# Stacking the last 16 keys' value products, spreading the rotary keys over 128 partitions and issuing the branch loads later, in a four-mixer decoder layer on one core

## The chip, the core and the metric

The kernel runs on 1 core of one Trainium2 chip. The metric is the device time of one execution in microseconds (us). Three runs of the kernel before took 991.82, 991.32 and 989.41 us (median 991.32). A difference of about 0.3% is what a measurement of this kernel can tell from none.

## The reference, cut to what matters

One decoder layer on 1040 positions: 16 learned meta tokens, then 1024 of the sequence, each of width 1024. `NM` is 16, `L` is 1040, `H` is 8 heads.

```
h = rms_norm(x);  z = h @ w_in                       # all branch inputs and gates
y_a = pool_mixer(...)  @ w_out_pool
y_b = attention(...)   @ w_out_mla                   # 8 heads, 64 + 32 rotary dims, values of 64
y_c = conformer_conv(...) @ w_out_conf
y_d = short_conv(...)  @ w_out_sc
m = sum_i sigmoid(g_i) * y_i
out = (x + rms_norm(m @ w_o))[16:]
```

The attention is causal: query q sees the meta tokens and the sequence up to itself. The last 16 keys of a block of 512 queries are seen by its last 16 queries alone, because the meta tokens shift keys against queries by 16. The rotary part of the key (32 dims) is one for all heads.

Every float32 product is made of three TensorE products of split operands: with x = xh + xl and w = wh + wl it is wh·xh + wh·xl + wl·xh (the halves are of type float32r). So each block of values costs three products, too.

## The kernel before, in words

**Stages.** (1) About 0 to 645 us: x is normalised and transposed, and w_in is multiplied in "units" of seven products each with DVE, ACT and POOL evacuating; between the units the pumps advance the other work (convolutions, pooling, query, key and value projections, weight splits), whose results go to DRAM. (2) 645 to 858 us: attention, 8 heads in two halves of 512 queries, and between its products the 48 "fills", the output projections of the three other branches. (3) The rest: the attention's output projection and w_o.

**Order of the work.** The program is recorded first, and `Plan.flush` (line 355) then deals it out: each engine takes, at each planned time, the ready operation with the lowest priority number. Costs and landing times are its own estimates; `plan.behind()` (line 268) makes an operation wait in the plan for the last recorded TensorE operation, or for a given one; nothing on the chip waits for that, it only sets the order on the queue. `plan.ahead(n)` moves priorities. SP issues nearly all loads in this order, one after the other, and an issue whose semaphore isn't there holds all behind it.

**Attention** (`attend`, line 1438). For each block `j` of 128 keys: three score products into a bank of tag "s" (five banks), a mask on DVE, Exp on ACT into `p32`, a split into a high part (ACT copy) and a low part (POOL subtraction) in `pt`, and three value products into the one bank "o": `v_[:, j, :P]` (64 values, high part, and 64 ones, which sum the rows) with the high and the low part, then `v_[:, j, P:]` (low part of the values) with the high part (lines 1463 to 1465). For the last block the same happens on 16 keys and 16 queries. The maximum of each row is put into four extra rows of the query tile `qt`, by a transpose and a DVE multiplication with `negd` (line 1432); scores of a half can't start before this.

**Between stages 1 and 2.** The last unit's four gate outputs go through three buffers `z` and are stored to `th` by POOL (line 752, `g == 30`). DVE's last evacuation, `z<-ps_pc`, needs the buffer of the first of them, so it waits for that store to land; DVE's two `qt` operations stand behind it. Meanwhile SP loads: queries, masks, keys and values of two heads, and the first branch's operands `bo` (two of 1 MB, `load_bo(0)`, line 1524), weights `whl` and gates `th` for the first fill.

**Rotary keys** (`task_kv`, line 1207): on 32 partitions of 1040 columns, two products with the cosine and sine tables, a sum, and a split, POOL doing four of the five operations. At the same time DVE halves parts of the parameter table `par` (line 904), in place.

Of the kernel before, what the change touches and what calls it, by code (L numbers as in the profile page):

```python
# [21 lines left out]
F32 = mybir.dt.float32  # L22
# [8 lines left out]
P = 128  # L31
# [40 lines left out]
def f(ap):  # L72
    return ap.bitcast(F32)
# [385 lines left out]
def trunk_kernel(ctx, tc, a):  # L459
# [56 lines left out]
    q_dram = [dram.tile([H, QK, 2, 512], F32R, name=f"q{c}") for c in range(2)]  # L516

    k_dram = [dram.tile([P, 2, L], F32R, name=f"k{g}") for g in range(4)]
    kr_dram = dram.tile([32, 2, L], F32R, name="kr")

    v_dram = [dram.tile([4, P, 9, 192], F32R, name=f"v{g}") for g in range(2)]
    l_dram = [dram.tile([NT], F32, name=f"l{h}") for h in range(H)]
    r_dram = [dram.tile([NT], F32, name=f"r{h}") for h in range(H)]

    mask_dram = [dram.tile([P, P], F32, name=f"mask{i}") for i in range(2)]
    negd_dram = dram.tile([4, 4, P], F32, name="negd")
# [27 lines left out]
    def t4(shape, dt=F32, name="t4"):  # L554
        return tp.tile(shape, dt, tag="t4", bufs=4, name=name)
# [345 lines left out]
    PE.transpose(pt[:, :NPAR], prow[:NPAR, :], ident[:NPAR, :NPAR])  # L901
    DVE.tensor_copy(par[:, :NPAR], pt[:, :NPAR])
    for r0, r1, n in ((R_DW, R_DW, 62), (R_GB, R_GB, 32), (R_HLB, R_LB, 2)):
        DVE.tensor_scalar(par[:, r0:r0 + n], par[:, r1:r1 + n], 0.5, None, op0=ALU.mult)

# [38 lines left out]
    def task_consts():  # L944

        for i in range(2):
            mask = w1([P, P], name="mask")
            causal(mask, 1 - 2 * i)
            ld(mask_dram[i], mask)
        t = t4([4, L], name="kone")  # L950
        POOL.memset(t, 1.0)
        ld(ones_dram, t)
        t = t4([4, 4, P], name="negd")
        POOL.memset(t, -1.0)
        POOL.affine_select(out=t, in_=t, compare_op=ALU.is_equal, fill=0.0,
                           base=0, pattern=[[-1, 4], [0, P]], channel_multiplier=1)
        ld(negd_dram, t)
        yield

    def k_rows(k_, h, part):  # L960

        e = h % 2
        ld(k_[:64], part(k_dram[h // 2][64 * e:64 * (e + 1)]))
        if h < 2:
            for r in range(2):
                ld(k_[64 + 16 * r:80 + 16 * r], part(kr_dram[16 * (r ^ e):16 * (r ^ e) + 16]))

    def row_maxima(c, mx, q_, k_, mask, bank):

# [236 lines left out]

    def task_kv():

        k0, k1, cs = t4([32, L], name="kr0"), t4([32, L], name="kr1"), t4([32, L], name="kcs")
        for k_, r0, i in ((k0, 0, 0), (k1, 32, 1)):  # L1210
            ld(k_, z_dram["kr"][r0:r0 + 32, :])
            ld(cs, a["trig"][i][:32, :])
            mul(POOL, k_, k_, cs)
            cs = t4([32, L], name="kcs2") if i == 0 else None
        add(POOL, k0, k0, k1)
        yield
        kh = t4([32, L], F32R, name="krh")
        copy(kh, k0)
        ld(kr_dram[:, 0], kh)
        kl = t4([32, L], F32R, name="krl")  # L1220
        sub(POOL, kl, k0, f(kh))
        ld(kr_dram[:, 1], kl)
# [12 lines left out]
        yield  # L1235
        for g in range(4):
            wk = w1([P, P], name="wk")
            ld(wk.rearrange("p (h c) -> p h c", c=64),
               w_ukv[:, 2 * P * g:2 * P * (g + 1)].rearrange("p (h c) -> p h c", c=P)[:, :, :64])
            whl = w1([P, 2, P], F32R, name="wkhl")  # L1240
            split(whl[:, 0], whl[:, 1], wk)
            yield
            for n0, n in CH_L:
                ps = bank()[:, :n]
                PE.matmul(ps, whl[:, 0], ch[:, n0:n0 + n], start=True, stop=False)
                PE.matmul(ps, whl[:, 0], cl[:, n0:n0 + n], start=False, stop=False)
                PE.matmul(ps, whl[:, 1], ch[:, n0:n0 + n], start=False, stop=True)
                hl = t4([P, 2, 348], F32R, name="khl")[:, :, :n]
                copy(hl[:, 0], ps)
                sub(DVE, hl[:, 1], ps, f(hl[:, 0]))  # L1250
                ld(k_dram[g][:, :, n0:n0 + n], hl)
                yield
        for g in range(2):
            wv = w1([P, 4, 64], name="wv")
            ld(wv, w_ukv[:, 4 * P * g:4 * P * (g + 1)].rearrange("p (h c) -> p h c", c=P)[:, :, 64:])
            whl = w1([P, 2, 256], F32R, name="wvhl")
            split(whl[:, 0].rearrange("p (h c) -> p h c", c=64), whl[:, 1].rearrange("p (h c) -> p h c", c=64), wv)
            yield
            for j in range(9):
                n = P if j < 8 else NM  # L1260
                ps = bank()[:n, :256]
                s_ = slice(P * j, P * j + n)
                PE.matmul(ps, ch[:, s_], whl[:, 0], start=True, stop=False)
                PE.matmul(ps, ch[:, s_], whl[:, 1], start=False, stop=False)
                PE.matmul(ps, cl[:, s_], whl[:, 0], start=False, stop=True)
                p3 = ps.rearrange("p (h c) -> p h c", c=64)
                hl = t4([P, 4, 192], F32R, name="vhl")[:n]
                POOL.memset(f(hl[:, :, 64:128]), 1.0)
                copy(hl[:, :, :64], p3)
                sub(DVE, hl[:, :, 128:], p3, f(hl[:, :, :64]))  # L1270
                ld(v_dram[g][:, :n, j].rearrange("h p c -> p h c"), hl)
                yield
# [113 lines left out]
    negd = qk.tile([4, 4, P], F32, name="negd")  # L1386
    NA = QK + 4
    qt = {}

# [3 lines left out]

    load_q(0, 0)
    kt = [qk.tile([NA, 2, LK], F32R, name=f"kt{i}") for i in range(2)]
    vt = [qk.tile([P, 9, 192], F32R, name=f"vt{i}") for i in range(2)]
    for t, src in ((maskS, mask_dram[0]), (maskT, mask_dram[1]), (negd, negd_dram),
                   *((kt[i][QK:NA, 0, :L], ones_dram) for i in range(2))):
        ld(t, src)

# [8 lines left out]
    def load_v(h):  # L1409
        v_ = vt[h % 2]  # L1410
        v = v_dram[h // 4][h % 4]
        ld(v_[:, 0:8].rearrange("p j c -> p (j c)"), v[:, 0:8].rearrange("p j c -> p (j c)"))
        ld(v_[:NM, 8], v[:NM, 8])

    def maxima(h, c):

        q_, k_ = qt[h, c], kt[h % 2]  # L1420
# [11 lines left out]
        DVE.tensor_tensor(q_[QK:NA, 0, :].rearrange("p (r n) -> p r n", n=P),  # L1432
                          pm[:4, :P].unsqueeze(1).to_broadcast([4, 4, P]), negd, op=ALU.mult)
        yield

    ol = {}
# [1 line left out]
    def attend(h, c):  # L1438
# [4 lines left out]
        for j in range(nj):  # L1443
# [15 lines left out]
            pt_ = at.tile([P, 2, 512], F32R, tag="pt", bufs=4, name="pt")[:kn, :, :n]  # L1459
            ACT.activation(p32, s, AF.Exp)  # L1460
            split(pt_[:, 0], pt_[:, 1], p32)
            o = po[:, lo_ - 512 * c:]
            PE.matmul(o, v_[:kn, j, :P], pt_[:, 0], start=(j == 0), stop=False, skip_group_check=True)
            PE.matmul(o, v_[:kn, j, :P], pt_[:, 1], start=False, stop=False, skip_group_check=True)
            PE.matmul(o[:64], v_[:kn, j, P:], pt_[:, 0], start=False, stop=(j == nj - 1), skip_group_check=True)
            yield
        if c == 0:
            ol[h] = at.tile([P, 2, 512], F32, tag="ol", bufs=2, name="ol")
# [47 lines left out]
    def fills():  # L1516
# [322 lines left out]
```

## Time and profile before

| What | us |
|---|---|
| three runs | 991.82, 991.32, 989.41; median 991.32 |
| the profiled execution, its own time | 990.85 |
| its span, from the first to the last instruction | 989.0 |
| TensorE (PE) busy | 969.4 (98%) |
| VectorE (DVE), GpSimd (POOL), ScalarE (ACT) busy | 696.8, 692.7, 444.0 |
| mean granted TensorE clock | 0.993 |

The 1.85 us between span and time lie around the program. A row of the timeline gives start, length, engine, tile written and tiles read, shape and count; what stands in brackets is the idle time before and what ended it. L353 is the line that issues all planned operations, so groups are told apart by tile names. PEld is the weight load of a product; matmuls are pipelined, so the start of one to the start of the next is its price, not its own length.

### The profile page before, as it was taken

How to read it: one execution, taken by the hardware profiler on the slowest of the kernel's cores; microseconds unless marked ns; L12 is line 12 of the kernel's file. 1: busy time of each engine (PE TensorE's matmuls, PEld its weight loads, DVE VectorE, ACT ScalarE, POOL GpSimd, SP SyncE). 2: the span in 40 equal slices, each digit the busy share in tenths (PEclk: the TensorE clock that was granted, in tenths of full speed). 3: DMA queues.
4: the chain of work that ended last, by engine and by line, in shares of the span. 5: the costliest groups of instructions: out<-in, count | busy, mean ns of one | idle time of the engine just before them, and what ended most of it. 6: DMA issues, size and time to landing. Idle time of an engine off the chain costs nothing. (4 is left out here: it accounts for less than half of the span.)

```text
span 989.0 us, 15388 instructions
## 1 busy us (share of the span) xinstructions
PE 969.4 (98%) x5095; PEld 824.6 (83%) x5095; DVE 696.8 (70%) x1109; ACT 444.0 (45%) x898; POOL 692.7 (70%) x630
## 2 busy tenths in 40 slices
PE   9999999999999999999999999989999999999996
PEld 8998899889888887888887888868888888788885
DVE  5948966979988965555365677236776687799747
ACT  7644243344344554554344344356455554224631
POOL 5848665558777787996599788345468795647956
PEclk9999999999999999999999999989999999999998
DMA  7144567667778687777647787778778674772634
GB/s 253 35 113 129 170 203 233 217 210 243 218 261 266 191 249 218 230 228 223 183 133 215 239 273 257 198 276 280 202 184 271 187 193 129 253 249 90 202 112 170
DMA packets 134551, 202.30 MB, mean 205 GB/s; under 512 B 20262, under 2 KB 81309, under 8 KB 133704
## 3 DMA queue, kind: packets, MB, share of 16 engines
q1 hardware_dynamic: 125496, 184.54, 60.8%
q10 hardware_dynamic: 8656, 15.74, 4.4%
q8 instruction: 40, 0.66, 0.3%
q0 software_dynamic: 320, 1.05, 0.3%
q14 instruction: 39, 0.32, 0.1%
HBM read 128.48 MB, written 72.81 MB: 204 GB/s over the span
## 5 line engine op out<-in xcount | busy, mean ns | idle before, releaser
L353 PE MATMUL ps_pb<-T,S 128*128 128x512 f32 (+2 forms) x792 | 171.6, 358 | 2.0 <-DVE u L353 2.0
L353 PE MATMUL ps_pa<-B,A 128*128 128x512 f32 (+2 forms) x792 | 170.4, 360 | 0.0
L353 PEld LDWEIGHTS ps_pb<-T,S 128*128 128x128 f32 x792 | 134.5, 189 | 23.7 <-DVE u L353 2.4
L353 PEld LDWEIGHTS ps_pa<-B,A 128*128 128x128 f32 x792 | 134.6, 188 | 22.8 <-issue 1.4
L353 POOL TENSOR_TENSOR S<-ss,S 128x512 fp32r<-128x512 f32 x84 | 114.5, 1376 | 49.0 <-ACT S L353 48.7
L353 POOL TENSOR_TENSOR A<-raw,A 128x512 fp32r<-128x512 f32 x84 | 114.6, 1370 | 39.2 <-ACT A L353 37.6
L353 POOL TENSOR_TENSOR pt<-p,pt 128x512 fp32r<-128x512 f32 (+4 forms) x112 | 105.6, 967 | 49.4 <-PE ps_s L353 31.5
L353 DVE TENSOR_TENSOR u<-ps_pb,u 128x512 f32<-128x512 f32 (+2 forms) x66 | 40.3, 611 | 78.2 <-PE ps_pb L353 71.6
L353 DVE SCALAR_TENSOR_TENSOR ps_w<-conv,par,ps_w 128x512 f32<-128x512 f32 x116 | 87.2, 752 | 2.6
L353 PE MATMUL ps_y<-bo,whl 128*128 128x512 f32 x288 | 87.1, 409 | 0.0
L353 PE MATMUL ps_pc<-B,S 128*128 128x512 f32 (+1 forms) x396 | 86.4, 359 | 0.0
L353 PE MATMUL ps_pd<-T,A 128*128 128x512 f32 (+2 forms) x396 | 85.2, 359 | 0.0
L353 PE MATMUL ps_pc<-T,S 128*128 128x512 f32 (+1 forms) x396 | 84.2, 358 | 0.0
L353 ACT ACTIVATE S<-ss 128x512 fp32r<-128x512 f32 x84 | 50.4, 627 | 68.5 <-DVE ss L353 37.3
L353 ACT ACTIVATE p<-ps_s 128x512 f32<-128x512 f32 (+4 forms) x112 | 49.4, 442 | 60.2 <-PE ps_s L353 34.9
L353 PEld LDWEIGHTS ps_pc<-B,S 128*128 128x128 f32 x396 | 67.0, 188 | 11.1 <-issue 0.5
L353 PEld LDWEIGHTS ps_pd<-T,A 128*128 128x128 f32 x396 | 67.0, 188 | 10.6
L353 PEld LDWEIGHTS ps_pc<-T,S 128*128 128x128 f32 x396 | 66.8, 189 | 10.7
L353 PE MATMUL ps_o<-pt,vt 128*128 128x512 f32 (+4 forms) x336 | 73.5, 329 | 0.4 <-ACT ol L353 0.4
L353 PE MATMUL ps_s<-qt,kt 100*128 100x512 f32 (+4 forms) x336 | 70.5, 333 | 0.3 <-DVE qt L353 0.3
L353 PEld LDWEIGHTS ps_o<-pt,vt 128*128 128x128 f32 (+1 forms) x336 | 54.4, 171 | 15.1 <-issue 1.3
L353 DVE TENSOR_TENSOR z<-ps_pc,u 128x512 f32<-128x512 f32 (+1 forms) x66 | 40.2, 609 | 37.3 <-PE ps_pc L353 27.3
(271 smaller groups left out, 1933.1 us busy)
## 6 DMA issues: line engine op xcount, KB each, us to landing
raw<-in_w_in_dram SPq DMA_DIRECT2D x52, 512.0 KB
th<-th SPq DMA_DIRECT2D x32, 512.0 KB
th<-z ACTq DMA_DIRECT2D x60, 256.0 KB
v<-vhl SPq DMA_DIRECT2D x16, 384.0 KB
qt<-q SPq DMA_DIRECT2D x16, 384.0 KB
vt<-v SPq DMA_DIRECT2D x8, 768.0 KB
bo<-bo SPq DMA_DIRECT2D x6, 1024.0 KB
kt<-k SPq DMA_DIRECT2D x8, 520.0 KB
```

Source lines behind the costliest of these rows:

```text
L353: getattr(self.handle[o["eng"]], o["op"])(*map(real, o["args"]), **{k: real(v) for k, v in o["kw"].items()})
```

## The change

Five edits. (a) In `attend`, the last 16 keys are taken apart from the full blocks: their probabilities are put into a tile `pz` of 80 rows, high part in rows 0 to 15, low part in 32 to 47, high part again in 64 to 79, zero between; the values into a tile `vs`, rows as they belong to these; one product of 80 rows takes the place of three of 16. ACT makes two copies where it made one. `vs` is loaded by three small loads for each head in place of one, and zeroed once by a load. (b) The rotary keys are worked on as 128 partitions of 260 columns, and stored as `[2, 32, L]`. (c) The halved parameters are read from the PSUM bank of the transpose, not from `par` itself. (d) `negd` is gone; the extra key rows are -1 and the diagonal is taken from `ident`. (e) `load_bo(0)` and the first fill's loads are planned behind the last TensorE operation recorded so far, and the second and third fill's behind the first fill's first product.

```diff
-    kr_dram = dram.tile([32, 2, L], F32R, name="kr")
+    kr_dram = dram.tile([2, 32, L], F32R, name="kr")
...
-        DVE.tensor_scalar(par[:, r0:r0 + n], par[:, r1:r1 + n], 0.5, None, op0=ALU.mult)
+        DVE.tensor_scalar(par[:, r0:r0 + n], pt[:, r1:r1 + n], 0.5, None, op0=ALU.mult)
...
-        k0, k1, cs = t4([32, L], name="kr0"), t4([32, L], name="kr1"), t4([32, L], name="kcs")
+        def rows32(x):
+            return x.rearrange("p (c n) -> (p c) n", c=4)
+        k0, k1, cs = (t4([P, L // 4], name=x) for x in ("kr0", "kr1", "kcs"))
         for k_, r0, i in ((k0, 0, 0), (k1, 32, 1)):
-            ld(k_, z_dram["kr"][r0:r0 + 32, :])
-            ld(cs, a["trig"][i][:32, :])
+            ld(k_, rows32(z_dram["kr"][r0:r0 + 32, :]))
+            ld(cs, rows32(a["trig"][i][:32, :]))
             mul(POOL, k_, k_, cs)
...
-    vt = [qk.tile([P, 9, 192], F32R, name=f"vt{i}") for i in range(2)]
+    vt = [qk.tile([P, 8, 192], F32R, name=f"vt{i}") for i in range(2)]
+    vs = [qk.tile([NS, 2, P], F32R, name=f"vs{i}") for i in range(2)]
+    pz = [at.tile([NS, NM], F32R, name=f"pz{i}") for i in range(3)]
...
+        e = v[:NM, 1:9].rearrange("p (c j) d -> p c j d", j=4)[:, :, 3]
+        for r, w in ((0, slice(0, P)), (32, slice(0, P)), (64, slice(P, 192))):
+            ld(vs[h % 2][r:r + NM, :, :w.stop - w.start], e[:, :, w])
         ld(v_[:, 0:8].rearrange("p j c -> p (j c)"), v[:, 0:8].rearrange("p j c -> p (j c)"))
-        ld(v_[:NM, 8], v[:NM, 8])
...
+            if kn == NM:
+                x = pz[(2 * h + c) % 3]
+                copy(x[:NM], p32)
+                copy(x[64:], p32)
+                sub(POOL, x[32:32 + NM], p32, f(x[:NM]))
+                PE.matmul(o, vs[h % 2][:, c], x, start=False, stop=True, skip_group_check=True)
+            else:
...
-        bos = {}
-        load_bo(0)
+        bos, begun = {}, []
+        with plan.behind():
+            load_bo(0)
...
-                with plan.behind() if d + bi else nullcontext():
+                with plan.behind(begun[0] if 0 < d + bi < 3 else None):
                     whl = wtile(fp, wname, d, 0)
                     ld(th, th_dram[8 * gi + d])
+                begun.append(len(plan.ops))
```

The plan deals the work out anew, so rows move on all engines from about 80 us on. Three places matter in what follows.

SP at the start of attention, from the second head's keys (`kt_6900`, now `kt_6905`) on. Before:

```order
L353 DMA kt_6900<-kr 16x2x1040 x2
L353 DMA bo<-bo_5246 128x2048
L353 DMA bo<-bo_5777 128x2048
L353 DMA whl<-w_out_pool_715 128x512
L353 DMA th<-th_3932 128x1024
L353 DMA vt_6931<-v_2504 128x1536
L353 DMA vt_6931<-v_2504 16x192
L353 DMA qt<-q_5072 96x1024
L353 DMA whl<-w_out_pool_1051 128x512
```

And now:

```order
L354 DMA kt_6905<-kr 16x2x1040 x2
L354 DMA vs_6903<-v_2483 16x2x128 x2
L354 DMA vs_6903<-v_2483 16x2x64
L354 DMA vt_6931<-v_2483 128x1536
L354 DMA qt<-q_5254 96x1024
L354 DMA bo<-bo_5184 128x2048
L354 DMA bo<-bo_5695 128x2048
L354 DMA whl<-w_out_pool_715 128x512
L354 DMA th<-th_3935 128x1024
L354 DMA qt<-q_4075 96x1024
```

The branch operands stood ahead of the second head's values; now they stand behind them and behind the fourth query load, which waits for a query buffer to come free.

PE at the same place: `ps_s<-ident,mrs` are the transposes for the first head's row maxima, `ps_s<-qt,kt` scores, `ps_s<-kt,qt` the second head's row maxima, `ps_o` value products, `ps_y<-bo` a fill. Before:

```order
L353 MATMUL ps_s<-ident,mrs 4x128 x2
L353 MATMUL ps_s<-kt_6900,qt 128x144
L353 MATMUL ps_s<-kt_6900,qt 128x272
L353 MATMUL ps_s<-kt_6900,qt 128x400
L353 MATMUL ps_s<-qt,kt_6898 128x512 x3
L353 MATMUL ps_s<-qt,kt_6898 128x400 x3
L353 MATMUL ps_s<-qt,kt_6898 128x272 x3
L353 MATMUL ps_s<-qt,kt_6898 128x144 x3
L353 MATMUL ps_s<-qt,kt_6898 16x16 x3
L353 MATMUL ps_o<-pt,vt_6905 128x512
L353 MATMUL ps_y<-bo,whl 128x512 x2
```

And now:

```order
L354 MATMUL ps_s<-ident,mrs 4x128 x2
L354 MATMUL ps_s<-qt,kt_6899 128x512 x3
L354 MATMUL ps_s<-qt,kt_6899 128x400 x3
L354 MATMUL ps_s<-qt,kt_6899 128x272 x3
L354 MATMUL ps_s<-qt,kt_6899 128x144 x3
L354 MATMUL ps_s<-qt,kt_6899 16x16 x3
L354 MATMUL ps_s<-kt_6905,qt 128x144
L354 MATMUL ps_o<-pt,vt_6913 128x512
L354 MATMUL ps_s<-qt,kt_6899 128x512 x5
L354 MATMUL ps_o<-pt,vt_6913 128x512
```

The three row maxima ahead of the first scores have moved behind them, and the first fill, which came 10 rows behind the transposes, now comes 50 rows behind them, after 77 products.

DVE in stage 1, around the halving of `par` (`u<-ps_pb` is the evacuation for which a unit's next product waits). Before:

```order
L353 COPY par<-ps_x 128x111
L353 TENSOR_SCALAR par<-par 128x62
L353 SCALAR_TENSOR_TENSOR z<-z 128x272
L353 TENSOR_TENSOR z<-ps_pc,u_1059 128x256
L353 SCALAR_TENSOR_TENSOR z<-z 128x256
L353 TENSOR_SCALAR par<-par 128x32
L353 TENSOR_TENSOR u_1187<-ps_pb,u_1163 128x256
L353 TENSOR_SCALAR par<-par 128x2
```

And now:

```order
L354 COPY par<-ps_x 128x111
L354 TENSOR_SCALAR par<-ps_x 128x62
L354 TENSOR_SCALAR par<-ps_x 128x32
L354 TENSOR_SCALAR par<-ps_x 128x2
L354 SCALAR_TENSOR_TENSOR z<-z 128x272
L354 TENSOR_TENSOR z<-ps_pc,u_1059 128x256
L354 SCALAR_TENSOR_TENSOR z<-z 128x256
L354 TENSOR_TENSOR u_1184<-ps_pb,u_1165 128x256
```

All three halvings now follow the copy at once, and none stands beside the two `u` evacuations of the next unit.

More of the change, by code (lines that the diff above doesn't have):

```diff
@@ L47 @@
 LH = 512 + NM
+NS = 5 * NM
 LK, LR = 1088, 576
@@ L525, in trunk_kernel @@
     mask_dram = [dram.tile([P, P], F32, name=f"mask{i}") for i in range(2)]
-    negd_dram = dram.tile([4, 4, P], F32, name="negd")
+    zero_dram = dram.tile([NS, 2 * P], F32, name="zero")
     ones_dram = dram.tile([4, L], F32, name="ones4")
@@ L950, in task_consts @@
         t = t4([4, L], name="kone")
-        POOL.memset(t, 1.0)
+        POOL.memset(t, -1.0)
         ld(ones_dram, t)
[L953 to L957, printed above, removed]
+        t = t4([NS, 2 * P], name="zero")
+        POOL.memset(t, 0.0)
+        ld(zero_dram, t)
         yield
@@ L965, in k_rows @@
             for r in range(2):
-                ld(k_[64 + 16 * r:80 + 16 * r], part(kr_dram[16 * (r ^ e):16 * (r ^ e) + 16]))
+                ld(k_[64 + 16 * r:80 + 16 * r], part(kr_dram[:, 16 * (r ^ e):16 * (r ^ e) + 16].rearrange("s p n -> p s n")))
     def row_maxima(c, mx, q_, k_, mask, bank):
@@ L1207, in task_kv @@
     def task_kv():
-        k0, k1, cs = t4([32, L], name="kr0"), t4([32, L], name="kr1"), t4([32, L], name="kcs")
+        def rows32(x):
+            return x.rearrange("p (c n) -> (p c) n", c=4)
+        k0, k1, cs = (t4([P, L // 4], name=x) for x in ("kr0", "kr1", "kcs"))
         for k_, r0, i in ((k0, 0, 0), (k1, 32, 1)):
-            ld(k_, z_dram["kr"][r0:r0 + 32, :])
-            ld(cs, a["trig"][i][:32, :])
+            ld(k_, rows32(z_dram["kr"][r0:r0 + 32, :]))
+            ld(cs, rows32(a["trig"][i][:32, :]))
             mul(POOL, k_, k_, cs)
-            cs = t4([32, L], name="kcs2") if i == 0 else None
+            cs = t4([P, L // 4], name="kcs2") if i == 0 else None
         add(POOL, k0, k0, k1)
         yield
-        kh = t4([32, L], F32R, name="krh")
+        kh = t4([P, L // 4], F32R, name="krh")
         copy(kh, k0)
-        ld(kr_dram[:, 0], kh)
-        kl = t4([32, L], F32R, name="krl")
+        ld(rows32(kr_dram[0]), kh)
+        kl = t4([P, L // 4], F32R, name="krl")
         sub(POOL, kl, k0, f(kh))
-        ld(kr_dram[:, 1], kl)
+        ld(rows32(kr_dram[1]), kl)
         yield
@@ L1385, in trunk_kernel @@
     maskS, maskT = (qk.tile([P, P], F32, name=n) for n in ("maskS", "maskT"))
-    negd = qk.tile([4, 4, P], F32, name="negd")
     NA = QK + 4
@@ L1395, in trunk_kernel @@
     kt = [qk.tile([NA, 2, LK], F32R, name=f"kt{i}") for i in range(2)]
-    vt = [qk.tile([P, 9, 192], F32R, name=f"vt{i}") for i in range(2)]
-    for t, src in ((maskS, mask_dram[0]), (maskT, mask_dram[1]), (negd, negd_dram),
+    vt = [qk.tile([P, 8, 192], F32R, name=f"vt{i}") for i in range(2)]
+    vs = [qk.tile([NS, 2, P], F32R, name=f"vs{i}") for i in range(2)]
+    pz = [at.tile([NS, NM], F32R, name=f"pz{i}") for i in range(3)]
+    for t in pz:
+        POOL.memset(f(t), 0.0)
+    for t in vs:
+        ld(t.rearrange("p c n -> p (c n)"), zero_dram)
+    for t, src in ((maskS, mask_dram[0]), (maskT, mask_dram[1]),
                    *((kt[i][QK:NA, 0, :L], ones_dram) for i in range(2))):
@@ L1432, in maxima @@
         DVE.tensor_tensor(q_[QK:NA, 0, :].rearrange("p (r n) -> p r n", n=P),
-                          pm[:4, :P].unsqueeze(1).to_broadcast([4, 4, P]), negd, op=ALU.mult)
+                          pm[:4, :P].unsqueeze(1).to_broadcast([4, 4, P]),
+                          ident[:4, :4].unsqueeze(2).to_broadcast([4, 4, P]), op=ALU.mult)
         yield
@@ L1458, in attend @@
             p32 = at.tile([P, 512], F32, tag="p32", bufs=3, name="p32")[:kn, :n]
-            pt_ = at.tile([P, 2, 512], F32R, tag="pt", bufs=4, name="pt")[:kn, :, :n]
             ACT.activation(p32, s, AF.Exp)
-            split(pt_[:, 0], pt_[:, 1], p32)
             o = po[:, lo_ - 512 * c:]
-            PE.matmul(o, v_[:kn, j, :P], pt_[:, 0], start=(j == 0), stop=False, skip_group_check=True)
-            PE.matmul(o, v_[:kn, j, :P], pt_[:, 1], start=False, stop=False, skip_group_check=True)
-            PE.matmul(o[:64], v_[:kn, j, P:], pt_[:, 0], start=False, stop=(j == nj - 1), skip_group_check=True)
+            if kn == NM:
[5 more added lines that the diff above has]
+            else:
+                pt_ = at.tile([P, 2, 512], F32R, tag="pt", bufs=4, name="pt")[:, :, :n]
+                split(pt_[:, 0], pt_[:, 1], p32)
+                PE.matmul(o, v_[:, j, :P], pt_[:, 0], start=(j == 0), stop=False, skip_group_check=True)
+                PE.matmul(o, v_[:, j, :P], pt_[:, 1], start=False, stop=False, skip_group_check=True)
+                PE.matmul(o[:64], v_[:, j, P:], pt_[:, 0], start=False, stop=False, skip_group_check=True)
             yield
```

## The prediction

> **What bounds the kernel now.** I read the page first, for the busy shares, then the busy time by stretch.
>
> ```profile
> span 989.0 us, 15388 instructions
> PE 969.4 (98%) x5095; PEld 824.6 (83%) x5095; DVE 696.8 (70%) x1109; ACT 444.0 (45%) x898; POOL 692.7 (70%) x630
> ...
> 645.00:657.40 12.40, 8.56 (x30) 6.52 (x29) 4.77 (x14) 3.45 (x7) 2.96 (x4) 0.72 1.02 395
> 657.40:820.00 162.60, 162.60 (x867) 135.49 (x866) 112.92 (x283) 91.41 (x208) 118.64 (x119) 1.00 0.73 211
> ```
>
> TensorE is the bound: 969.4 of 989.0 us, and in steady attention 162.60 of 162.60, at full clock. There a product removed is time removed, and other engines' work counts only where PE waits for it. The first stretch is the exception: PE is busy 8.56 of 12.40 us, and the clock (third number from the end) is 0.72. So next I read PE's waits, and around these the timeline.
>
> ```profile
> PE ps_s L353 <- DVE z L353: 3.4, 1, 3.4
> PE ps_pb L353 <- DVE u L353: 2.0, 2, 1.5
> ```
>
> Of some 20 us in which PE isn't busy, these two waits are those that the change touches; the others lie at the program's start and end. 0.3% of the time is 3.0 us, and that is what a measurement can tell from no change.
>
> **Part A, the last 16 keys: -4.2 us.** Sixteen halves of attention each lose three products of 16 rows and gain one of 80. The last unit of the program shows the price, and a product of 128 rows with a single column bounds the new one.
>
> ```profile
> 851.66 0.33 PE L353 MATMUL ps_o<-pt,vt 16*128 16x16 f32 x2
> 851.92 0.50 PE L353 MATMUL ps_y<-bo,whl 128*128 128x512 f32 x1
> ...
> L353 PE MATMUL ps_x<-ones,sqk 128*128 128x1 f32 x16 | 1.9, 240 | 0.0
> L353 ACT ACTIVATE pt<-p 16x16 fp32r<-16x16 f32 x16 | 3.4, 214 | 4.3 <-PE ps_o L353 4.1
> ```
>
> Two small products start at 851.66 and the next work at 851.92, so each holds PE for 0.13 us, whatever its 16 columns. One with 128 rows and one column takes 1.9 / 16 = 0.12, so rows cost nothing either, and I price the new one at 0.13. Two fewer in each of 16 halves: 16 x 2 x 0.13 = 4.2 us, all on the path, since PE is full there. Bounds: 3.2 if the 80-row one took 0.19, and 4.5 if 0.11. ACT's second copy adds 16 x 0.21 = 3.4 us to an engine at 45%. The one product must wait for POOL's difference, as the second of the three did, so that wait is not new. Two more small loads a head are issued on SP, ahead of loads of a later head: at no cost while those are a head early (their price if that cover went is in Part C).
>
> **Part B, rotary keys and parameters: -2.0 us.**
>
> ```profile
> 77.72 4.96 POOL L353 TENSOR_TENSOR kr<-kr,kcs 32x1040 f32<-32x1040 f32 x2
> 82.75 2.43 POOL L353 TENSOR_TENSOR kr<-kr,kr 32x1040 f32<-32x1040 f32 x1
> 85.15 0.73 POOL L353 TENSOR_TENSOR whl<-wraw,whl 128x256 fp32r<-128x256 f32 x1
> 86.79 2.45 POOL L353 TENSOR_TENSOR krl<-kr,krh 32x1040 fp32r<-32x1040 f32 x1 [0.25 <-PE ps_pc L353]
> ...
> 73.83 0.27 DVE L353 COPY par<-ps_x 128x111 f32<-128x111 f32 x1
> 77.95 2.37 DVE L353 TENSOR_SCALAR par<-par 128x32 f32<-128x32 f32 x1
> 80.58 2.13 DVE L353 TENSOR_SCALAR par<-par 128x2 f32<-128x2 f32 x1
> ...
> 80.71 1.69 PE L353 MATMUL ps_pb<-T,S 128*128 128x256 f32 x12 [1.53 <-DVE u L353]
> 91.64 1.58 PE L353 MATMUL ps_pb<-T,S 128*128 128x256 f32 x11 [0.48 <-DVE u L353]
> ```
>
> A multiplication of 32 columns by a number takes DVE 2.37 us, and one of 2 columns 2.13, just while POOL works on the 1040 rotary columns; the copy of 111 columns from PSUM took 0.27. DVE's evacuation `u` stands behind the first, and PE waits 1.53 us for it; behind `krl`, another `u` is late and PE waits 0.48. Now the three halvings read PSUM and come early, each bounded by the copy's 0.27, and POOL's four operations have 260 columns, priced by the 256-column row at 0.73 in place of 2.43 to 2.48. Both waits should go: 1.53 + 0.48 = 2.0 us. What is late next is PE itself: no other wait of this place stands among its waits. Bounds: 0 if the new order puts another slow DVE operation before a `u`, and 2.5 with what DVE's delay costs inside a product. Keys are needed only in attention, so the smaller packets of their loads and stores (1040 bytes a row in place of 4160) are hidden by hundreds of us.
>
> **Part C, the start of attention: -0.6 us.** These rows are SP's, POOL's, DVE's and PE's.
>
> ```profile
> 636.95 1.23 SPq L353 DMA_DIRECT2D bo<-bo  x2
> 640.88 3.21 SPq L353 DMA_DIRECT2D vt<-v  x2
> 653.72 0.32 SPq L353 DMA_DIRECT2D qt<-q  x1
> ...
> 639.34 0.76 POOL L353 DMA_DIRECT2D th<-z  x1 [11.35 <-ACT z L353]
> 650.25 0.54 POOL L353 DMA_DIRECT2D th<-z  x1 [6.42 <-ACT z L353]
> ...
> 648.50 0.69 DVE L353 TENSOR_TENSOR z<-ps_pc,u 128x512 f32<-128x512 f32 x1 [8.23 <-DMA th<-z]
> 649.23 1.28 DVE L353 TENSOR_TENSOR qt<-ps_s,negd 4x512 fp32r<-4x512 f32 x2
> ...
> 642.10 2.88 PE L353 MATMUL ps_pc<-B,S 128*128 128x512 f32 x12
> 644.82 0.38 PE L353 MATMUL ps_s<-ident,mrs 128*4 128x128 f32 x2
> 645.40 0.47 PE L353 MATMUL ps_s<-kt,qt 96*128 96x144 f32 x2 [0.20 <-PE ps_s L353]
> 649.25 0.45 PE L353 MATMUL ps_s<-kt,qt 96*128 96x400 f32 x1 [3.38 <-DVE z L353]
> 649.97 3.73 PE L353 MATMUL ps_s<-qt,kt 100*128 100x512 f32 x15 [0.26 <-DVE qt L353]
> ```
>
> The chain is: POOL's store of the first `z`, issued at 639.34, has landed at 648.50, 9.2 us later; then DVE's `z` (0.69) and first `qt` (half of 1.28), and at 649.97 the first scores, 1.5 us behind the landing. PE has nothing from about 645.9 to 649.25. Then the clock falls. The next fence has the stretches of it, and the last products of the program for comparison; ahead of them the load queue's packets between 640 and 645.7, and between 643.3 and 651 those of both queues (q0 is POOL's).
>
> ```profile
> q1 hardware_dynamic: 282, 1.28, 102.1%
> ...
> q1 hardware_dynamic: 294, 2.08, 73.5%
> q0 software_dynamic: 215, 0.75, 23.9%
> ...
> 643.50:646.93 3.43, 2.18 (x11) 1.37 (x9) 0.00 (x0) 0.00 (x0) 0.33 (x1) 1.00 0.95 326
> 646.93:650.34 3.41, 0.83 (x3) 0.52 (x4) 1.80 (x3) 0.72 (x1) 0.09 (x1) 1.00 0.99 413
> 650.34:657.17 6.83, 6.83 (x24) 5.52 (x23) 2.97 (x12) 2.73 (x6) 2.87 (x4) 0.50 1.03 384
> 977.99:981.40 3.41, 1.42 (x12) 1.22 (x11) 3.38 (x7) 1.59 (x6) 2.62 (x3) 1.00 0.41 154
> 981.40:989.00 7.60, 0.00 (x0) 0.00 (x0) 4.41 (x8) 0.14 (x2) 2.86 (x3) 0.50 0.65 242
> ```
>
> PE had 0.83 of 3.41 us to do, and the next 6.83 ran at 0.50: 3.4 us lost on top of the wait. At the end 1.42 of 3.41 was followed by half clock too, while 2.18 of 3.43 wasn't.
>
> What the change moves: `bo`, `whl` and `th` go behind the second head's values and a query load that SP could not issue before 653.72. So 2 MB less stand in the queue when the store goes out. Up to 645.7 the queue holds the same keys as before, and the store's packets don't show there at all (q1 alone, at 102.1%); its wait for a first packet is thus not made by `bo`. What `bo` can cost is the store's own passage after that: some 0.75 MB of q0 for three stores beside 73.5% of q1. I take 1.0 us off the landing: a store of 0.25 MB took a third of 7.7 us, 2.6, at a share of 23.9%, and with twice the share would take 1.3.  Bounds: 0, and 3 if the store waits for the whole queue to drain. So the first scores start at about 649.0. The three row maxima that used the gap now come later; at full clock a column costs 2.72 us / (12 x 512) (twelve products from 642.10 to 644.82), and their 816 columns 0.4 us. Net -1.0 + 0.4 = -0.6. From 645.3 to 649.0 PE then has nothing for 3.7 us, as long as before, so I leave half clock in.
>
> The Trainium skill, "DMA: Bandwidth & Descriptors", section on queues, rings and completion order, says that a DMA engine takes turns between the queues with work, packet by packet. By it a store is never held behind a full load queue, and holding `bo` back would gain next to nothing: the sum would end 1.0 us later. The trace agrees only in part, since q0 shows nothing until 645.7.
>
> New wait: the first fill. Between the first score and it stand 77 products of 27,384 columns: 12 us at full clock, 15.5 with half clock. Its loads go out behind the query load, 3.75 us after the first score (653.72 against 649.97); 0.4 + 2.0 + 0.25 MB at 2.08 MB in 7.7 us is 9.8, with 1 us to land 14.6. Hidden, by about 1 us; full clock would leave 2.6 us open, less what it saves. Part A's two extra loads of the first heads are issued here too, at half of 1.23 us each by `bo`'s row: up to 1.2, beside a queue that is full.
>
> **The sum.** The profiled execution took 990.85 us (span 989.0, 1.85 around it), 0.47 under the median of 991.32. 990.85 - 4.2 - 2.0 - 0.6 = 984.0.
>
> **The rivals.**
>
> *The clock stays up.* If the store lands by 646, the first scores start at 647.5, 2.4 us earlier, and the gap is 2.2: by the rows above not enough to drop the clock unless one window holds it all. It saves 2.4 - 0.4 + 3.4 = 5.4 in place of 0.6: 979.2. For it: 2 MB fewer in the queue. Against it: q0's absence before 645.7, when the queue is as before; the fourth store, issued at 650.25 beside a full queue too, has nothing of `bo` to blame. Chance 0.22. The Trainium skill, "TensorE: Matmul & The Clock Gate", section "Why this matters for your kernels", puts the limit at PE-idle gaps of about 3 us; by that rule a gap of 2.2 would keep the clock up, and my 3.7 would not.
>
> *The branch operands come late (the other side).* PE's queue is in order, so a first fill without operands stops everything behind it, scores too. The margin is 1 us. The page's rate by slices shows how it could go:
>
> ```profile
> GB/s 253 35 113 129 170 203 233 217 210 243 218 261 266 191 249 218 230 228 223 183 133 215 239 273 257 198 276 280 202 184 271 187 193 129 253 249 90 202 112 170
> ```
>
> At the 129 GB/s of a slice in attention, 2.65 MB take 20.5 us in place of 9.8: 10.7 later, 9.7 beyond the margin, and half clock again, 3.4: 984.0 + 13.1 = 997.1. It decides from 1 us of lateness, and cancels the whole gain at a lateness of 4.4 (3.4 + 3.4 = 6.8). Against it: around 650 the queue moves 384 to 413 GB/s. Chance of more than +3 us against before 0.04, of cancelling most 0.08.
>
> *It doesn't do what it says.* PE may wait at the small product for POOL in place of issuing three, or B's waits may return elsewhere in the new order; at half of A and B, 990.85 - 3.1 = 987.7. Against it: PE has no such wait in 162.60 us. Chance 0.08.
>
> **How the numbers follow.** Forecast 0.58 (984.0), clock 0.22 (979.2), late operands 0.12 (988 to 997), half effect 0.08 (987.7). The range runs from 979.0 to 988.0: below it lies little of the clock case, above it most of the late one. Faster by over 0.3% is under 988.3: 0.58 + 0.22 + most of the half effect, 0.86; within 0.3% 0.10; slower 0.04.
>
> **What would show it.** 16 products from `pz` with starts 0.13 us after the last one's; no 2 us `par` rows on DVE and no `ps_pb <- DVE u` wait near 80 and 91 us; the first store landed near 647.4, first scores near 1.5 us behind it (less 2 us for B), and a stretch at clock 0.50. It is wrong if the clock stays at 1.00 there, if `ps_y` waits for a DMA, or if the stretch from 657 to 820 us shrinks by less than 3 us.

## The result, and the profile after

| | before | changed |
|---|---|---|
| median (us) | 991.24 (989.41 to 991.82, 4 runs) | 984.06 (983.37 to 985.18, 4 runs) |
| ratio | | 0.9932, 95% interval 0.9915 to 0.9949 |
| profiled execution, its span | 990.85, 989.0 | 983.37, 981.2 |

The change saves 7 us; 984.0 was forecast. The terms of the sum were not those of the forecast, though. First the busy shares on the page of the changed kernel.

```profile
PE 961.4 (98%) x5063; PEld 819.9 (84%) x5063; DVE 689.3 (70%) x1109; ACT 449.1 (46%) x914; POOL 679.2 (69%) x632
```

What TensorE waits for, by the view of the waits (us in total, times, longest):

```profile
PE ps_s L354 <- DVE qt L354: 5.1, 1, 5.1
PE ps_y L354 <- DVE lcp L354: 1.4, 2, 1.0
...
PE ps_o L354 <- ACT ol L354: 1.3, 2, 0.8
PE ps_y L354 <- DVE th L354: 0.5, 2, 0.3
```

TensorE's busy time fell by 8.0 us and it is still the bound. The two waits for `u` are gone. The wait before the first scores has grown, from 3.4 for `z` to 5.1 for `qt`; `th` is waited for anew, and `ol` for longer (0.4 before).

**The last 16 keys.** Two timelines of the same place, before (eight products of the last blocks of the first half, then the next score) and after (five and the stacked one).

```profile
659.46 1.03 PE L353 MATMUL ps_o<-pt,vt 128*128 128x272 f32 x8
660.41 0.50 PE L353 MATMUL ps_s<-qt,kt 96*128 96x512 f32 x1
```

```profile
655.13 0.66 PE L354 MATMUL ps_o<-pt,vt 128*128 128x272 f32 x5
655.63 0.22 PE L354 MATMUL ps_o<-pz,vs 80*128 80x16 f32 x1
655.70 0.48 PE L354 MATMUL ps_s<-qt,kt 96*128 96x512 f32 x1
```

From start to start the eight held TensorE for 0.95 us and the six hold it for 0.57: 0.38 saved in this half. The stacked product takes 0.07, not 0.13.

Eleven of the sixteen halves of before looked like this one. In the other five the plan had parted the three small products, and there they cost more: a lone one 0.20, and the product ahead of each group is lengthened, too. This is so at the place from which the forecast took its price:

```profile
850.64 1.09 PE L353 MATMUL ps_y<-bo,whl 128*128 128x512 f32 x4
```

The four products ahead of the two small ones (at 851.66) hold TensorE for 1.02 us, and 0.91 is what four of 512 columns take (twelve take 2.72). Added up over all starts of the two timelines, the 48 small products of before held TensorE for 6.4 us and lengthened those ahead of them by 2.3; the sixteen stacked ones hold it for 1.1 and lengthen nothing. So the products gave some 7.5 us, where 4.2 was forecast.

**The rotary keys and parameters.** TensorE at the parameters' transpose (of before, then of after) and at the second of the `ps_pb` products that had waited, and VectorE's three halvings.

```profile
71.66 0.26 PE L353 MATMUL ps_x<-ident,prow 111*128 111x111 f32 x1
```

```profile
70.48 0.26 PE L354 MATMUL ps_x<-ident,prow 111*128 111x111 f32 x1
...
88.04 1.60 PE L354 MATMUL ps_pb<-T,S 128*128 128x256 f32 x12
...
72.95 0.39 DVE L354 TENSOR_SCALAR par<-ps_x 128x62 f32<-128x62 f32 x3
```

The halvings take 0.39 us together, where two of them took 2.37 and 2.13. The second product starts at 88.04 and not at 91.64, 3.6 earlier, but 1.18 of that is there already at the transpose, ahead of every edit. That leaves 2.4 us.

**The start of attention.** From the timeline, GpSimd's first store and TensorE's first scores:

```profile
635.32 0.76 POOL L354 DMA_DIRECT2D th<-z  x1 [11.35 <-ACT z L354]
...
646.31 3.94 PE L354 MATMUL ps_s<-qt,kt 100*128 100x512 f32 x15 [5.13 <-DVE qt L354]
```

From the busy time by stretch (PE first, the clock third from the end), the stretch that was too empty and the one at half clock:

```profile
639.96:643.37 3.41, 1.22 (x7) 0.67 (x5) 0.00 (x0) 0.00 (x0) 0.00 (x0) 1.00 1.04 253
643.37:653.61 10.24, 7.30 (x24) 6.21 (x25) 3.83 (x10) 3.77 (x8) 3.81 (x8) 0.50 0.56 201
```

And from the DMA view, the first store alone, then the fourth (KB, us from issue to landing):

```profile
th<-z POOLq DMA_DIRECT2D x1, 256.0 KB, 9.4
...
th<-z POOLq DMA_DIRECT2D x1, 256.0 KB, 2.3
```

The store lands 9.4 us after its issue, not earlier than before (9.0), the scores still come 1.6 us behind that, and 7.3 us of work run at half clock (6.8 before). This place has given nothing.

### The profile page after: what moved, and what is told of

Read it like the earlier page. It is cut to its first block, busy times and chain, and to the rows that moved or that the text cites. A ratio compares the mean times of both kernels' runs of the same rounds, so it can differ in the third digit from the quotient of the medians.

```text
span 981.2 us, 15371 instructions
## 1 busy us (share of the span) xinstructions
PE 961.4 (98%) x5063; PEld 819.9 (84%) x5063; DVE 689.3 (70%) x1109; ACT 449.1 (46%) x914; POOL 679.2 (69%) x632
## 4 chain that ended last, share of the span: by engine, by line
PE 91%; DVE 4%; DMA 3%; issue 1%; ACT 1%; SPq 0%; POOL 0%; DVEq 0%; POOLq 0%; ACTq 0%
PE ps_pb L354 16%; PE ps_pa L354 16%; PE ps_pc L354 15%; PE ps_o L354 9%; PE ps_pd L354 7%; PE ps_u L354 7%; PE ps_s L354 7%; PE ps_y L354 6%; PE ps_x L354 5%; PE ps_w L354 1%; DMA th<-z 1%; DMA kt<-k 1%; DMA vt<-v 1%; DVE th L354 1%; DVE a L354 1%
## 5 line engine op out<-in xcount | busy, mean ns | idle before, releaser
L354 POOL TENSOR_TENSOR pt<-p,pt 128x512 fp32r<-128x512 f32 (+1 forms) x96 | 101.5, 1080 | 44.1 <-PE ps_s L354 22.7
L354 PE MATMUL ps_y<-bo,whl 128*128 128x512 f32 x288 | 85.1, 404 | 0.2 <-DVE th L354 0.2
L354 PE MATMUL ps_s<-qt,kt 100*128 100x512 f32 (+4 forms) x336 | 70.8, 334 | 5.1 <-DVE qt L354 5.1
L354 PE MATMUL ps_o<-pt,vt 128*128 128x512 f32 (+7 forms) x288 | 68.3, 347 | 1.4 <-ACT ol L354 1.3
L354 PEld LDWEIGHTS ps_s<-qt,kt 100*128 100x128 f32 (+1 forms) x336 | 55.9, 183 | 15.1 <-DVE qt L354 5.4
```

Of the source, the lines that this page charges most:

```text
L354: getattr(self.handle[o["eng"]], o["op"])(*map(real, o["args"]), **{k: real(v) for k, v in o["kw"].items()})
```

## The experiments

Each time is the median of the runs, each ratio is to the kernel before on the same chip, with its 95% interval. Each edit lets the plan deal out the whole work anew, so a single edit also moves rows far away from it.

### Each edit group alone, and the change without the held loads

**e1_stack**: edits (a) and (d) on the kernel before.

> The kernel before with the stacked product alone (its tiles and loads, and the row maxima without the multiplier table). Theory from the two traces: a product of 16 rows costs more than its own 0.13 us, because the product ahead of it is lengthened from 0.066 to 0.160 us; with 80 rows that goes, and the stacked product itself costs 0.073. That is 16 x (0.160 + 0.132 + 0.112 + 0.127 - 0.066 - 0.073) = 6.3 us, of which new waits in attention may give 1 to 2 back: 985 to 987 us (ratio 0.9935 to 0.9960), with 0.07 us from one start to the next at each of the 16 stacked products. Rival, the forecast's price: 0.13 for each product, so 4.2 us saved: 987.0 us, and 0.13 from start to start. Second rival, the gain lies elsewhere: 991 us.

Measured 989.52, ratio 0.9983 (0.9974 to 0.9992): 1.7 us saved, less than any theory but the last. From start to start the stacked product takes the expected 0.07; the stretch at half clock and the first store's way to landing follow, each from its view.

```profile
660.70 0.22 PE L354 MATMUL ps_o<-pz,vs 80*128 80x16 f32 x1
660.77 1.18 PE L354 MATMUL ps_s<-qt,kt 96*128 96x512 f32 x4
```

```profile
649.05:659.29 10.24, 8.41 (x27) 7.13 (x28) 3.83 (x10) 4.29 (x11) 3.89 (x9) 0.50 1.03 379
```

```profile
th<-z POOLq DMA_DIRECT2D x1, 256.0 KB, 10.3
```

So the products' gain is there, and most of it is given back: the store lands 10.3 us after its issue (9.0 before), 8.4 us of work at half clock cost 0.8 more than the 6.8 of before do, and attention has new waits, the longest for the row maxima `mxs`.

**e2_rotpar**: edits (b) and (c) on the kernel before.

> The kernel before with the rotary keys on 128 partitions and the parameters halved from PSUM, and nothing else. Theory: the two waits of TensorE at 80 and 91 us go and with them 2.4 us (from the starts of the same products in both traces, 1.18 us of an earlier difference taken off): 988.8 us, ratio 0.9976. What came 1.18 us earlier already at 71 us is the landing of the input's third block, which no edit touches: it may fall either way in this profile. Rival: the change itself brings these 1.18 us: 987.6 us, ratio 0.9963, and TensorE at the transpose of the parameters by 70.5 us in place of 71.7. The forecast's number: 2.0 us, 989.2 us.

Measured 988.07, ratio 0.9971 (0.9959 to 0.9983): 2.9 us, which holds 2.4. The second product starts at 88.21, its transpose at 70.66: 2.4 us saved between the two, as in the full change. The parameters' transpose itself lies anywhere from 70.1 to 71.7 us in the profiles, and at 71.5 in e1_stack against 70.8 in e3_hold, neither of which changes anything ahead of it; the early 1.2 us is thus put down to the execution and not to the change.

**e3_hold**: edit (e) on the kernel before.

> The kernel before with the held loads alone (branch operands, and the first three fills' weights and gates). Theory: the first store of the last unit's gates lands 9.0 to 9.4 us after its issue as before, since its packets start only when the keys' loads ahead are through; the scores start no earlier, three row maxima come behind them (+0.4 us): 991.0 to 992.0 us, ratio 1.0000 to 1.0008; half clock stays. Rival, the forecast's term: landing 1.0 us earlier, 0.6 us saved: 990.6 us. Second rival, the clock stays up: 986 us.

Measured 996.27, ratio 1.0053 (1.0040 to 1.0066): 5.3 us slower, outside of every theory. The store lands 8.8 us after its issue, so the holds gain 0.2 there. The loss lies in attention, with these rows late in it (VectorE, GpSimd, TensorE), and the stretch of 3.41 us around them:

```profile
816.88 3.59 DVE L353 TENSOR_TENSOR m<-m,th 128x512 f32<-128x512 f32 x1
...
813.18 4.80 POOL L353 TENSOR_TENSOR pt<-p,pt 128x512 fp32r<-128x512 f32 x4
...
821.01 0.73 PE L353 MATMUL ps_s<-qt,kt 100*128 100x512 f32 x2 [2.38 <-DVE mxs L353]
```

```profile
818.25:821.66 3.41, 1.03 (x5) 0.56 (x4) 3.38 (x6) 0.23 (x2) 1.67 (x2) 1.00 0.24 77
```

VectorE's addition `m`, with both operands in SBUF, stands behind an unbroken row of GpSimd's for 3.59 us, the row maxima behind it come late, TensorE waits 2.38 us, is busy for 1.03 of 3.41, and the next 3.41 run at half clock (1.7 us lost). At the start of attention, too, half clock covers more work: 9.7 us from 647.58 to 657.82, against 6.8 before, which is 1.4 us more. These three make 5.5 us; what else moved was not taken apart.

**e4_nohold**: the changed kernel with edit (e) undone.

> The changed kernel without the held loads. Theory: the holds give nothing, so 983.0 to 984.3 us against 984.06 (ratio to the kernel before 0.992 to 0.993), the store landing 9.0 to 9.4 us after issue, the scores starting up to 0.4 us earlier. Rival, the forecast's term: the holds are worth 0.6 us: 984.7 us. Second rival: the holds avoid a late store: 986 us or more.

Measured 985.19, ratio 0.9942 (0.9928 to 0.9956). By the medians the holds are worth 1.1 us here, which the intervals don't tell from nothing. The first store's way:

```profile
th<-z POOLq DMA_DIRECT2D x1, 256.0 KB, 10.9
```

10.9 us with the stack and no holds (10.3 in e1_stack), 9.4 with both, 9.0 with neither, 8.8 with the holds alone: the stacked product's edit makes the store later, and the holds make up for a part of that.

### What the stacked product saves by

**e7_16row**: `PE.matmul(o, vs[h % 2][:NM, c], x[:NM], ...)` in place of all 80 rows.

> The changed kernel with the stacked product cut to its first 16 rows (the low parts of the last 16 keys are left out of the sums). As many products as in the changed kernel. Theory: a product of 16 rows is slow where one of 80 isn't: the product ahead goes from 0.066 to 0.160 us, and its own from start to start from 0.073 to 0.13: 16 x 0.15 = 2.4 us more than the changed kernel, 986.5 us. Rival, price by the number of products: no difference, 984.1 us, and start to start 0.07.

**e8_80x3**: the stacked product in a loop of three.

> The changed kernel with the stacked product issued three times (the last 16 keys' part is counted three times). As many products as before the change, each of 80 rows. Theory: each further product of 80 rows costs 0.07 to 0.11 us from start to start, and the product ahead keeps its 0.066: 16 x 2 x (0.07 to 0.11) = 2.2 to 3.5 us more than the changed kernel, 986.3 to 987.6 us. Rival, each product costs what one of 16 rows did (0.13, and 0.09 more for the product ahead): 16 x (2 x 0.13 + 0.06 + 0.09) = 6.6 us more, 990.7 us.

Measured 985.97 (ratio 0.9952, 0.9940 to 0.9964) and 985.49 (0.9947, 0.9935 to 0.9959). These intervals overlap that of the changed kernel, so the times decide nothing and the traces have to. The same place in both timelines, e7_16row first:

```profile
655.80 0.66 PE L354 MATMUL ps_o<-pt,vt 128*128 128x272 f32 x5
656.39 0.27 PE L354 MATMUL ps_o<-pz,vs 16*128 16x16 f32 x1
656.59 1.20 PE L354 MATMUL ps_s<-qt,kt 96*128 96x512 f32 x4
...
656.39 0.18 PEld L354 LDWEIGHTS ps_o<-pz,vs 16*128 16x128 f32 x1
```

```profile
656.58 0.66 PE L354 MATMUL ps_o<-pt,vt 128*128 128x272 f32 x5
657.07 0.44 PE L354 MATMUL ps_o<-pz,vs 80*128 80x16 f32 x3
657.37 1.17 PE L354 MATMUL ps_s<-qt,kt 96*128 96x512 f32 x4
```

The five products ahead take 0.59 us where a product of 16 rows follows, and 0.49 or 0.50 where one of 80 does; the 16-row one itself takes 0.20 and the 80-row ones 0.10 each in a row, 0.07 alone. All told: 0.95 us with three of 16 rows, 0.79 with one of 16, 0.79 with three of 80, 0.57 with one of 80. Fewer products alone and more rows alone each bring 0.16 of the 0.38. The weight load of 16 rows starts with its product (656.39 both), that of 80 rows 0.07 us ahead, beside the product before:

```profile
655.56 0.19 PEld L354 LDWEIGHTS ps_o<-pz,vs 80*128 80x128 f32 x1
```

### What the wait before the scores is worth

**e5_z4**: the first gate output of the last unit in a slot of its own.

```diff
...
+            if last and (i, j) == (0, 0):
+                z = wp.tile([P, n], F32, tag="blk", bufs=7, name="z")[:m, :nj]
...
```

> The changed kernel with the first of the last unit's four gate outputs in a buffer of its own (a slot of the weight blocks, which has no further use), so that VectorE's last evacuation waits for no store of that unit. Theory: the store's landing is what holds the scores. Without it the evacuation follows its product at 641 us and the first scores start at about 642.4 instead of 646.31, TensorE has nothing for some 1.2 us instead of 5.13, and the clock stays up, which is worth half of the 7.3 us of work at half clock: 3.9 + 3.65 = 7.5 us, so 976.5 us (ratio to the kernel before 0.985). Rival: a landing of the later stores, for whose buffers the tiles of probabilities wait, takes its place: 980 to 983 us, with the wait before a value product. Second rival: the clock drops all the same: 980 us, with the scores at 642.4.

Measured 980.34, ratio 0.9903 (0.9889 to 0.9917): faster than the kernel before, by the medians than the changed kernel too (the intervals just touch), and 3.8 us short of the theory. TensorE's row at the start, then VectorE's, GpSimd's and TensorE's late in attention, and three stretches:

```profile
642.39 2.27 PE L354 MATMUL ps_s<-qt,kt 100*128 100x512 f32 x15 [1.28 <-DVE qt L354]
...
801.73 4.57 DVE L354 TENSOR_TENSOR m<-m,th 128x512 f32<-128x512 f32 x1
...
798.51 4.82 POOL L354 TENSOR_TENSOR pt<-p,pt 128x512 fp32r<-128x512 f32 x4
...
806.84 0.59 PE L354 MATMUL ps_s<-qt,kt 100*128 100x400 f32 x1 [1.76 <-DVE mxs L354]
```

```profile
639.73:643.14 3.41, 2.13 (x11) 1.45 (x10) 1.97 (x3) 0.72 (x1) 0.54 (x2) 1.00 1.04 242
803.57:806.98 3.41, 1.65 (x8) 1.03 (x7) 3.41 (x4) 0.44 (x3) 2.18 (x3) 1.00 0.25 53
806.98:810.40 3.42, 3.42 (x12) 3.30 (x13) 3.29 (x10) 1.89 (x4) 1.41 (x2) 0.50 0.37 104
```

The start came out as expected, at 642.39 and at full clock. The gain of half clock was lost again later: `m` behind GpSimd for 4.57 us, TensorE without work for 1.76 and 3.41 us at half clock, as in e3_hold. Such a row doesn't always hold the addition that long: in the changed kernel the like addition took 1.07 us at 808.84, beside a row of 5.25.

**e6_actstore**: the last unit's stores on ScalarE's queue.

> The changed kernel with the last unit's four stores issued by ScalarE on its hardware queue in place of GpSimd's software queue. Theory: what delays the store is the full load queue, whatever the queue that the store stands in; its first packet comes 3 to 6 us after the issue, it lands 6 to 9.4 us after, the scores start at most 2 us earlier, and TensorE still has nothing for over 3 us: 982 to 984.5 us. Rival: the software queue itself is slow; a hardware store lands within 4 us, VectorE's evacuation waits at most 1 us, the scores start by 643 and the clock stays up: 977 us.

Measured 998.04, ratio 1.0085 (1.0070 to 1.0100). Neither theory foresaw it. SP's and TensorE's waits, the former over the start of attention:

```profile
SPq L354 <- DMA th<-z: 29.2, 6, 11.1
...
PE ps_s L354 <- DMA kt<-kr: 10.3, 1, 10.3
```

The loads of attention's tiles now wait for gate stores on SP, up to 11.1 us (3.6 in the changed kernel), and all keys come late. So the stores went out beside a load queue with little in it (q1 held 20.0% of the DMA engines from 632 to 645 us), and the run can't tell a slow software queue from a full load queue. Other profiles speak for the load queue. The changed kernel's fourth store, on the same software queue, landed in 2.3 us beside a load queue (q1) that held 1.3% of the DMA engines from 646.5 to 648.9, and the first of before took 9.0 behind one at 102.1%. The holds show it with little else changed: by the same view the fourth store took 6.7 us before and 2.3 with the holds alone (e3_hold), 6.5 in e4_nohold and 2.3 with the holds again.

```profile
q1 hardware_dynamic: 6, 0.01, 1.3%
```

**e9_z4_psum**: on e5_z4, the third branch's `m` takes its second operand from PSUM.

```diff
...
-                        DVE.scalar_tensor_tensor(t, t, 1.0, py, op0=ALU.add, op1=ALU.mult)
-                        add(POOL if bi == 1 else DVE, m_[c][d], m_[c][d], t)
+                        g = t if bi == 1 else py
+                        DVE.scalar_tensor_tensor(g, t, 1.0, py, op0=ALU.add, op1=ALU.mult)
+                        add(POOL if bi == 1 else DVE, m_[c][d], m_[c][d], g)
...
```

> The run e5_z4 with one more change: in the third branch's fills VectorE writes the gated product into its PSUM bank and adds it to m from there, so that this addition has one operand from SBUF and not two. Theory: in e5_z4 the addition m of 4.57 us (1.15 in the mean) stood behind GpSimd's unbroken row of operations at 798.5 to 804.6, since both its operands are in SBUF; from PSUM each takes 0.6 to 0.7, TensorE's wait of 1.76 us for the row maxima behind it goes, and the half clock of 3.41 us that followed goes too: 980.3 - 1.8 - 1.7 = 976.9 us (ratio to the kernel before 0.986). Rival: an addition waits for GpSimd wherever its operands are: no change, 980.3 us. Second rival: the bank is held longer and TensorE waits for it before fills: 981 us or more.

**e10_z4_nohold** and **e11_z4_psum_nohold**: e5_z4 and e9_z4_psum with edit (e) undone.

> The run e5_z4 without the held loads. Theory: the holds work through the load queue ahead of the four stores alone. Without them the first store lands 10.9 us after its issue, near 646.2; VectorE no longer waits for it, but ScalarE's third tile of probabilities does, which is due near 645: TensorE waits 1 to 2 us before a value product: 981.3 to 982.3 us. Rival: with VectorE's wait gone the holds are worth nothing: 980.3 us or less.

> The run e9_z4_psum without the held loads. Theory: as e9_z4_psum, plus the 1 to 2 us that e10_z4_nohold is expected to lose: 978 to 979 us. Rival, the holds are worth nothing here: 976.9 us or less.

Measured, in the order e9, e10, e11: 981.97 (0.9917, 0.9904 to 0.9929), 980.87 (0.9912, 0.9899 to 0.9925) and 985.24 (0.9954, 0.9939 to 0.9968). The mechanism of e9_z4_psum holds and its gain doesn't. The additions `m` of VectorE in attention, of e5_z4 and of e9_z4_psum (us, mean ns), and what TensorE waits for in the latter:

```profile
L354 DVE TENSOR_TENSOR m<-m,th 128x512 f32<-128x512 f32 x16 | 18.4, 1149 | 0.4
```

```profile
L354 DVE TENSOR_TENSOR m<-m,ps_y 128x512 f32<-128x512 f32 x16 | 11.0, 686 | 0.6
```

```profile
PE ps_o L354 <- ACT ol L354: 3.3, 3, 2.0
PE ps_y L354 <- DVE lcp L354: 1.9, 2, 1.0
PE ps_y L354 <- DVE m L354: 1.2, 3, 0.8
```

With one operand in PSUM the addition takes 0.69 us and not 1.15, and the late wait of 1.76 is gone, but the bank is waited for (1.2), as the second rival had it, and `ol` and `lcp` for 5.2, against 2.7 in e5_z4. Without the holds, e5_z4 is as fast as with them, within the intervals; the wait before a value product that was expected of it did not come, half clock did (the last section). e11_z4_psum_nohold is 3.3 us slower than e9_z4_psum, so there the holds count, by more than the theory had; why was not followed.

### The parameters alone

**e12_par**: edit (c) on the kernel before.

> The kernel before with the parameters halved from PSUM alone; GpSimd's rotary operations stay on 32 partitions of 1040 columns. Theory: an operation of VectorE with SBUF operands alone waits while GpSimd works, and these long ones are what it waits for. The three halvings leave that place, so the wait of 1.53 us at 80 us shrinks or goes, but VectorE's other operations still stand behind GpSimd (2.31 us for one z beside the last rotary operation), and the wait of 0.48 us stays: 0.5 to 1.5 us saved, 989.3 to 990.3 us. Rival: the halvings themselves are the cause, both waits go: 988.4 us, as with the rotary keys changed too.

Measured 996.07, ratio 1.0062 (1.0050 to 1.0074): 6 us slower, outside of both theories. Both waits at 80 and 91 us are gone: the second product starts 17.56 us behind the transpose (87.66 and 70.10), as in the full change. So the halvings alone take away both, as the rival had it, and nothing of these 2.4 us needs the rotary keys' edit. But other waits have come, first this one (VectorE, GpSimd, TensorE):

```profile
88.52 4.27 DVE L353 TENSOR_TENSOR raw<-raw 128x512 f32<-128x512 f32 x1
...
89.70 2.53 POOL L353 TENSOR_TENSOR S<-ss,S 128x512 fp32r<-128x512 f32 x2
...
93.65 1.70 PE L353 MATMUL ps_pc<-B,S 128*128 128x256 f32 x12 [1.38 <-DVE z L353]
```

An operation that takes 0.69 us in the changed kernel, where GpSimd is idle at this place (80.80 to 86.30), took 4.27 here, where `krl` (2.91 us) and what stands behind it fill it; `z` came 1.38 late. By these rows, what the rotary keys' edit adds is a free GpSimd. Some of the loss is of this kind; the rest lies in later waits of the new order, which were not taken apart.

## Why the prediction held, point by point

*Part A, -4.2: right in kind, mis-sized.* The price of 0.13 for the new product, and "rows cost nothing either", were the step that failed. Few rows cost: the product ahead of a 16-row one takes 0.09 more, which the sum left out, and an 80-row one takes 0.07. The products gave some 7.5 us, outside of the bounds 3.2 and 4.5. The Trainium skill, "TensorE: Matmul & The Clock Gate", section "Step-by-step: what each phase is for", says that TensorE pulls a weight load ahead of products in flight, where the row groups don't conflict or a background buffer takes it, and that a load's time doesn't go by the number of rows. The runs agree on the load's own length (0.18 us for 16 rows, 0.19 for 80) and show a limit of the pulling ahead: the 16-row load started only with its product, the 80-row one 0.07 us ahead. Why is not shown.

*Part B, -2.0: right, though by one of its two edits.* Between the starts it gave 2.4 us, inside the bounds 0 and 2.5, and alone 2.9 (1.7 to 4.1 by its interval). By e12_par the halvings from PSUM bring all of the 2.4, and the shorter rotary rows keep the next operations from waiting. The cause is the one named: VectorE's operations on SBUF alone wait while GpSimd works, here and in e3_hold, e5_z4 and e12_par. The Trainium skill, "SBUF — State Buffer", section "SBUF: two separate sides", has the two engines share a pair of ports that one instruction holds to its end, for VectorE's operations with two SBUF inputs among others. The runs agree for `m` (4.57 us, and 0.69 with one input in PSUM), and show a wait through more than one of GpSimd's instructions: the 4.57 us began beside its row of 4.82 and outlasted it. The lower bound "0 if the new order puts another slow DVE operation before a `u`" held for the two edits together, but such an order can cost more than that: with edit (c) alone it cost 6 us.

*Part C, -0.6: wrong.* "I take 1.0 us off the landing" failed: it came 0.4 later. What was held back is worth 1.5 us of landing (10.9 to 9.4), but edit (a) alone had made it 1.3 later (9.0 to 10.3). Its small loads were priced in Part A as issues on SP alone, "at no cost while those are a head early"; that it is these loads which fill the queue ahead of the store is argued and was not tried by itself. The rest of this part held: scores some 1.5 us behind the landing, half clock, and a first fill that waits for no DMA.

*New waits in attention, not forecast:* `ol`, `lcp` and `th` cost TensorE 3.2 us in place of 1.4. By the same view of before, `lcp` was 1.0 and `ol` 0.4. The forecast priced the order of before with some of its products taken out; the plan's new order was another.

*The sum.* From the first profile to the second the span falls by 7.8 us and the execution's own time by 7.5. By the starts of the same rows: -1.2 of the execution's own start, -2.4 for B, -0.4 for two small waits of stage 1 that are gone, +0.4 for the store, -7.5 for A's products, +0.4 for the row maxima behind the first scores, and +3.0 in the rest of attention: -7.7. Of these 3.0 the view of the waits gives 2.0 and half clock 0.2; the others were not taken apart. The forecast of -6.8 came near the total by errors that cancelled: A 3.3 and B 0.4 too small, C 1.4 too good, attention's 3.0 left out, and the start's 1.2 and the two small waits were luck.

*The rivals.* The late operands did not come: TensorE's waits name no DMA of `bo`, `whl` or `th` (the 1 us to land in their sum stands on no row). The clock stayed up there only in runs with the store off the chain (e5_z4, e9_z4_psum, e11_z4_psum_nohold; not e10_z4_nohold), and in e5_z4 attention took its gain back. The half effect is e1_stack's case, where the products' gain and the time part.

## What to carry to other kernels

A product of 16 rows was dear twice, in its own time (0.11 to 0.20 us, where one of 80 rows took 0.07 to 0.11) and in that of the product ahead (0.09 more), so try to stack small contractions (80 rows did it here; nothing between 16 and 80 was tried). When an edit takes work away, ask which queue its new transfers join and whose store stands behind them: with edit (a) alone, part of the gain was given back at a buffer's release of 10 us. An operation of VectorE with SBUF operands alone can take over five times its length beside an unbroken row of GpSimd's (3.59 to 4.57 us in place of 0.69); read it from the row that is longer than its like, and keep such a one off the chain. Where an edit makes a planner deal again, its price alone says little about its price with others: the holds cost 5.3 us alone and nothing that the intervals show on top of the two other groups.

## What the runs showed of the hardware

Half clock needs no long gap. In all profiles of this study the clock changes only at the bounds of a fixed grid of stretches of 3.41 us (half clock lasts 3.41, 6.83, 10.24 us and so on). From full clock it fell, with one exception, after stretches in which TensorE was busy for 1.65 us or less, and not after 1.73 or more; a wait of 1.76 us was enough. The exception is in e10_z4_nohold, whose rows show both sides:

```profile
641.94:645.35 3.41, 2.13 (x14) 1.86 (x13) 2.56 (x6) 1.32 (x2) 0.82 (x5) 1.00 1.02 245
645.35:648.77 3.42, 2.83 (x12) 2.29 (x12) 1.23 (x5) 1.84 (x4) 2.26 (x2) 0.50 1.01 419
...
969.62:973.03 3.41, 1.73 (x15) 1.52 (x13) 3.38 (x8) 1.30 (x5) 2.32 (x4) 1.00 0.41 154
973.03:976.44 3.41, 0.00 (x0) 0.00 (x0) 3.38 (x7) 0.44 (x2) 3.17 (x3) 1.00 0.61 231
```

2.13 busy there, half clock next, while the same 2.13 in e5_z4 kept it up. Why is open. The Trainium skill, "TensorE: Matmul & The Clock Gate", section "Why this matters for your kernels", puts the limit at idle gaps of about 3 us; these runs put it near half of a stretch.
